# RWKV preparation: head sums as 64x64 products on four quarters of the array, transposes of the values after the gram products

## The chip, the cores and the metric

The program runs on one NeuronCore of one Trainium2 chip. A core has five engines with queues of their own: TensorE (PE in the profile; PEld are its weight loads), VectorE (DVE), ScalarE (ACT), GpSimd (POOL) and SyncE (SP), which starts most of the weight transfers. The metric is the device time of one execution in microseconds. The kernel before takes 837.95 us, the median of 3 runs (837.28 to 838.62).

## The reference

The program computes one decoder block on 512 tokens of width 1024, in float32: an attention sub-layer made of a sparse attention mixer and an RWKV-7 mixer side by side, and a gated MLP. The change touches the preparation of the RWKV mixer, which has 8 heads of 64 channels:

```python
w = -jax.nn.softplus(-(w0 + jnp.tanh(xw) @ w2)) - 0.5
decay = jnp.exp(-jnp.exp(w.astype(jnp.float32)))
a = jax.nn.sigmoid(a0 + xa @ a2)
...
kk = k * k_k.reshape(H, N).astype(jnp.float32)
kk = kk / jnp.maximum(jnp.sqrt(jnp.sum(kk * kk, axis=-1, keepdims=True)), 1e-12)
k = k * (1.0 + (a - 1.0) * k_a.reshape(H, N).astype(jnp.float32))
...
y = y + jnp.sum(r * k * r_k, axis=-1, keepdims=True) * v
```

Two of these lines sum over the 64 channels of a head: the norm of `kk`, and the bonus `sum(r * k * r_k)`, which multiplies `v`. These are the head sums.

## The kernel before

Activations are kept with channels on the partitions and the 512 tokens along the free dimension. A tile of 128 partitions therefore holds two heads, a *pair*; there are four pairs (`NH2 = 4`). Every weight is split into two parts, `whi` and `wlo` (ACT rounds `raw` to `whi`, DVE or POOL subtracts to get `wlo`), as is the normalised input (`hh`, `hl`), and a projection of 128 channels (`dense_fm`, L417) is 24 matmuls of 128x128 by 512 columns into one PSUM bank: `whi` with `hh` and `hl` eight times, then `wlo` with `hh` eight times.

For each pair `p` the preparation has these steps:

- `front(p)` (L495): the projection of the key; two small products `zw` and `za` (64 rows each, side by side in the array) for decay and `a`; `shift_mix` writes `kx`; then the running sum `cum` of the log decay inside each chunk of 64 tokens, and its exponentials `ep` and `pi`.
- `norms(p)` (L519): ACT squares `kx` into `kk`; TensorE multiplies `kk` by `ones`, a 128x128 matrix with two 64x64 blocks of ones on its diagonal, so that each partition receives the sum over its own head; DVE bounds it from below (`rn`), ACT takes logarithm and exponential, which makes 1/norm.
- `receptance(p)` (L531) and `values_of(p)` (L536): one projection each, into `rx` and `vx`. There is one buffer for `vx`.
- `values_tok(p)` (L541): four 128x128 transposes of `vx` on TensorE, and four copies by ACT into `UV` (values with tokens on the partitions).
- `vectors(p)` (L551): ten DVE instructions that build `AR`, `bh` and `tv`; TensorE sums `tv` over each head with the same `ones`, and DVE multiplies the sums by `vx` into `BO`.
- `gram(p)` (L570): sixteen transposes of `bh` into two banks, copied by ACT into `BKT`; then for each of eight chunks and both heads a product of `bh` with `AR`, masked by DVE into `AB`. The first four chunks go into one bank each of the tags `b` and `a`, the last four into two banks of the tag `mm`.

PSUM has eight banks: four with the tag `mm` (`mmb()`), two with `a` (`pa()`) and two with `b` (`pb()`). Tiles of one tag take their turns on its banks, so that a tile waits until the one before it on that bank has been read for the last time.

The loop at L597 to L609 works on two pairs at a time: `front` and `norms` of pair p+1, then `values_tok` and `vectors` of pair p, `receptance` of p+1, `gram` of p, `values_of` of p+1. Behind the third round comes one more projection (`kcp`). This part is not ordered by hand: a planner at compile time sets the order of each engine's queue, by the order of the program, by when it expects operands to be ready, and by free banks and buffers. `tc.high_priority()` moves the instructions in its block to the front of that choice. Other parts stand under `tc.manual_schedule`, which keeps the written order on the engines named.

After the loop DVE inverts the 32x32 diagonal blocks of all chunks (L625 to L636), a long run of dependent instructions, beside which TensorE makes the query and key projections. The chunk recurrence follows from L941 on; it uses products of 64x64 on all four quarters of the array (L951 and L954: `AR` with the state `M0` into the banks X and Y).

Of the kernel before, what the change touches and what calls it, by code (L numbers as in the profile page):

```python
# [13 lines left out]
AF = mybir.ActivationFunctionType  # L14
ALU = mybir.AluOpType
# [8 lines left out]
DH = 64  # L24
H = 8
NH2 = H // 2
# [54 lines left out]
def hybrid_block(ctx: ExitStack, tc: tile.TileContext, A: dict, out: bass.AP):  # L81
# [25 lines left out]
    def bank(tag, bufs, shape=(128, 512)):  # L107
        return ps.tile(list(shape), F32, name="ps_" + tag, tag=tag, bufs=bufs)

    def mmb():  # L110
        return bank("mm", 4)

    def pa():
        return bank("a", 2)

    def pb():
        return bank("b", 2)

    def mm(o, l, r, start, stop):
        te.matmul(o, lhsT=l, rhs=r, start=start, stop=stop)  # L120

    def act(o, i, f=AF.Copy, **kw):
        sc.activation(o, i, f, **kw)  # L123

    def tt(o, a, b, op):
        v.tensor_tensor(o, a, b, op=op)  # L126

    def ts(o, a, s1, s2, op0=ALU.mult, op1=ALU.add):
        if s2 is None:
            v.tensor_scalar(o, a, s1, None, op0=op0)  # L130
        else:
            v.tensor_scalar(o, a, s1, s2, op0=op0, op1=op1)

    def stt(o, a, s, b, op0=ALU.mult, op1=ALU.add):
        v.scalar_tensor_tensor(o, a, s, b, op0=op0, op1=op1)  # L135
# [3 lines left out]
    ident, mask, ones, cmask = kc[:, 0:128], kc[:, 128:256], kc[:, 256:384], kc[:, 384:416]  # L139
# [16 lines left out]
    for name in ("rwkv_mu", "rwkv_w0", "rwkv_a0", "rwkv_k_k", "rwkv_k_a", "rwkv_r_k", "rwkv_ln_g", "rwkv_ln_b"):  # L156
        r0, n = ROWS[name]
        src = A[name]
        if name == "rwkv_r_k":
            src = src.rearrange("l h d -> l (h d)")  # L160
# [3 lines left out]
    pt = pa()  # L164
# [3 lines left out]
    def col(name, i=0):  # L168
        r0, n = ROWS[name]
        return prm[:, r0 + i:r0 + i + 1]  # L170
# [37 lines left out]
    def norm_tiles(pool_):  # L208
        return (cp.tile([128, NT, 2], F32, name="ss", tag="ss"),
                [pool_.tile([128, D], F32, name="h", tag="h", bufs=NT) for _ in range(NT)])  # L210
# [123 lines left out]
    with tc.manual_schedule(engines={getattr(mybir.EngineType, e) for e in ("PE", "Activation", "DVE", "Pool")}):  # L334
# [37 lines left out]
        for k in range(KT):  # L372
# [5 lines left out]
            if k == 6:  # L378
                pt = pa()
# [37 lines left out]
    def dense_fm(xh, xl, kt=KT):  # L417
        return run(dense_fm_g(xh, xl, kt))
# [12 lines left out]
    UV = rp.tile([128, NCH, NH2, 2, DH], F32, name="UV")  # L431
    BO = gp.tile([128, 4, S], F32, name="BO", tag="BO")
# [11 lines left out]
    def shift_mix(p, m, dst):  # L444
        mu = col("rwkv_mu", m)
        act(dst, p, AF.Copy, scale=omm[:, m:m + 1])
        stt(dst[:, 1:], p[:, :-1], mu, dst[:, 1:])

    def t2(name, bufs=1):
        return tp.tile([128, S], F32, name=name, tag=name, bufs=bufs)  # L450
# [11 lines left out]
    for name, (r0, n) in ROWS.items():  # L462
        if r0 >= NR0:
            r0 -= NR0
            src = A[name]
            if name.startswith("cmp_pe"):
                src = src.rearrange("l a d -> l (a d)")
# [10 lines left out]
    def chunks(ap):  # L478
        return ap.rearrange("p (c t) -> p c t", t=C)
# [15 lines left out]
    def front(p):  # L495
        cs = slice(128 * p, 128 * p + 128)
        kx = t2("kx", 2)
        pk = dense_fm(hh, hl)
        zw, za = pa(), pb()
        mm(zw, wa[0:64, cs], xw[0:64], True, True)  # L500
        mm(za, wa[64:128, cs], xw[64:128], True, True)
        shift_mix(pk, 4 + p, kx)
        cl = t2("cl")
        act(cl, zw, AF.Tanh, scale=0.5, bias=w0h[:, p:p + 1])
        aa = t2("aa", 2)
        act(aa, za, AF.Tanh, scale=0.5, bias=a0h[:, p:p + 1])
        ts(cl, cl, -0.5 * DECAY, -0.5 * DECAY)
        cum = t2("cum")
        v.tensor_tensor_scan(out=cum, data0=scanm.rearrange("p c t -> p (c t)"), data1=cl, initial=0.0,
                             op0=ALU.mult, op1=ALU.add)  # L510
        ep = tp.tile([128, NCH, C + 1], F32, name="ep", tag="ep", bufs=2)
        v.memset(ep[:, :, 0:1], 1.0)
        act(ep[:, :, 1:], chunks(cum), AF.Exp)
        pi = t2("pi", 2)
        act(pi, cum, AF.Exp, scale=-1.0)
        v.tensor_copy(PC[:, p, :, None], ep[:, :, C:C + 1])
        L[p] = dict(kx=kx, aa=aa, ep=ep, pi=pi)

    def norms(p):  # L519
        kx = L[p]["kx"]  # L520
        kk = t2("kk", 2)
        act(kk, kx, AF.Square, scale=col("rwkv_k_k", p))
        ss = pa()
        mm(ss, ones, kk, True, True)
        rn = t2("rn", 2)
        ts(rn, ss, 1e-24, None, op0=ALU.max)
        act(rn, rn, AF.Ln)
        act(rn, rn, AF.Exp, scale=-0.5)
        L[p].update(kk=kk, rn=rn)

    def receptance(p):  # L531
        rx = t2("rx", 2)
        shift_mix(dense_fm(hh, hl), p, rx)
        L[p]["rx"] = rx

    def values_of(p):  # L536
        vx = t2("vx")
        shift_mix(dense_fm(hh, hl), 8 + p, vx)
        L[p]["vx"] = vx

    def values_tok(p):  # L541
        vx = L[p]["vx"]
        pt = pb()
        for i in range(4):
            te.transpose(pt[:, 128 * i:128 * i + 128], vx[:, 128 * i:128 * i + 128], ident)
        for r in range(2):
            for cc in range(2):
                act(UV[64 - 64 * r:128 - 64 * r, cc::2, p, r, :],
                    pt[64 * cc:64 * cc + 64].rearrange("p (c r d) -> p c r d", r=2, d=DH)[:, :, r, :])

    def vectors(p):  # L551
        kx, aa, ep, pi, kk, rn, rx, vx = (L[p][k] for k in ("kx", "aa", "ep", "pi", "kk", "rn", "rx", "vx"))
        stt(AR[:, p, :, 1, :], chunks(rx), 1.0, ep[:, :, 1:], ALU.mult, ALU.mult)
        stt(kk, kx, col("rwkv_k_k", p), rn, ALU.mult, ALU.mult)
        stt(AR[:, p, :, 0, :], chunks(kk), -1.0, ep[:, :, 0:C], ALU.mult, ALU.mult)
        stt(kk, aa, 1.0, kk, ALU.add, ALU.mult)
        bh = tp.tile([128, NCH, 3, C], F32, name="bh", tag="bh")
        stt(bh[:, :, 0, :], chunks(kk), 0.5, chunks(pi), ALU.mult, ALU.mult)
        v.tensor_copy(bh[64:128, :, 2, :], bh[64:128, :, 0, :])
        ts(aa, aa, kah[:, p:p + 1], oma[:, p:p + 1])  # L560
        stt(kx, kx, 1.0, aa, ALU.mult, ALU.mult)
        stt(bh[:, :, 1, :], chunks(kx), 1.0, chunks(pi), ALU.mult, ALU.mult)
        tv = t2("tv")
        stt(tv, rx, col("rwkv_r_k", p), kx, ALU.mult, ALU.mult)
        L[p]["bh"] = bh
        bs = pa()
        mm(bs, ones, tv, True, True)
        tt(BO[:, p], bs, vx, ALU.mult)

    def gram(p):  # L570
        bh = L[p]["bh"]
        ptr = [pb(), pa()]
        for c in range(NCH):
            for r in range(2):
                rs = slice(64 * r, 64 * r + 64)
                te.transpose(ptr[r][:, 64 * c:64 * c + 64], bh[rs, c, r:r + 2].rearrange("p a t -> p (a t)"),
                             ident[rs, rs])
        for r in range(2):
            act(BKT[:, :, p, r, :], ptr[r].rearrange("p (c j) -> p c j", c=NCH))
        for c0 in range(0, NCH, 4):  # L580
            ptr = [mmb(), mmb()] if c0 else [pb(), pa()]
            for i in range(4):
                for r in range(2):
                    rs = slice(64 * r, 64 * r + 64)
                    mm(ptr[r][:, 128 * i:128 * i + 128], bh[rs, c0 + i, r:r + 2].rearrange("p a t -> p (a t)"),
                       AR[rs, p, c0 + i].rearrange("p a t -> p (a t)"), True, True)
            for r in range(2):
                tt(AB[:, c0:c0 + 4, p, r, :], ptr[r].rearrange("p (c t) -> p c t", c=4),
                   mask[:, None, :].to_broadcast([128, 4, 128]), ALU.mult)


    front(0)
    norms(0)
    receptance(0)
    values_of(0)
    late_params()
    for p in range(NH2):  # L597
        if p + 1 < NH2:
            front(p + 1)
            norms(p + 1)  # L600
        values_tok(p)
        vectors(p)
        if p + 1 < NH2:
            receptance(p + 1)
        gram(p)
        if p + 1 < NH2:
            values_of(p + 1)
        if p + 2 == NH2:
            kcp = dense_fm(hh, hl)  # L609
# [15 lines left out]
    for g in range(2):  # L625
        for b in range(2):
            r = 64 * g + 32 * b
# [75 lines left out]
    pt = pa()  # L703
# [31 lines left out]
    for b in (1, 0):  # L735
        for g in range(2):
            r = 64 * g + 32 * b
# [511 lines left out]
    for m in range(KT):  # L1249
        cs = slice(128 * m, 128 * m + 128)  # L1250
# [13 lines left out]
    ss, hs = norm_tiles(ntp)  # L1264
# [36 lines left out]
    with tc.manual_schedule(engines=KTS):  # L1301
        for t in range(NT):
            qs = slice(128 * t, 128 * t + 128)
            p = mmb()
# [13 lines left out]
        for pair in range(2):  # L1318
            cs = slice(256 * pair, 256 * pair + 256)
# [37 lines left out]
    for hf in range(2):  # L1357
        bo = dense_tok(512, aT[:, 0], aT[:, 1], NF)
        for t in range(NT):
            n = 256 if hf and t == NT - 1 else 512  # L1360
            for c0 in range(0, 512, n):
                cs = slice(512 * hf + c0, 512 * hf + c0 + n)
# [30 lines left out]
```

## Time and profile before

| | us |
|---|---|
| median of 3 runs | 837.95 |
| the profiled execution | 837.93 |
| its span, first to last instruction | 836.1 |
| TensorE busy | 822.2 |
| DVE busy | 514.2 |
| ACT busy | 406.7 |
| POOL busy | 52.4 |

All durations in rows are those of the one profiled execution. A row of the order of time has the start (us from the span's start), the busy time, the engine, the line of the code, the operation, the tile written and the tiles read, and shapes; `x8` at its end merges eight instructions. A float32 matmul appears as two instructions, since it makes two passes; the dense products, in the rounded type, appear as one. Matmul lines are those of the helper `mm` (L120), DVE and ACT lines often those of `tt` (L126), `ts` (L130), `stt` (L135) and `act` (L123), so the tiles' names tell the instructions apart. `ps_a`, `ps_b` and `ps_mm` are the banks by tag; `kc` is the constant tile that holds `ones` and the identity. A row that groups instructions has their number, their busy time, the mean of one in ns, and the engine's idle time before them with what ended it.

### The profile page before, as it was taken

The page shows a single profiled execution, that of the slowest core. Times are in us where ns is not written, and L with a number is a line of the kernel's source. Part 1 is how long each engine was busy: PE and PEld are TensorE (multiplying, and loading weights), DVE is VectorE, ACT ScalarE, POOL GpSimd, SP SyncE. Part 2 cuts the span into 40 slices and gives each one's busy share as a digit, 9 for nine tenths or more (in the row PEclk, how much of TensorE's full clock was granted, in tenths as well). Part 3 has the DMA queues.
Part 4 walks back from the last instruction along what each step waited for, and adds up shares of the span by engine and source line. Part 5 has one row for each costly group of instructions (what it writes and reads, how often), then busy time and mean ns, then how long its engine had stood idle before and what let it go on. Part 6 is the DMA issues. An engine that isn't in the chain of part 4 may idle for free.

```text
span 836.1 us, 12860 instructions
## 1 busy us (share of the span) xinstructions
PE 822.2 (98%) x5097; PEld 667.1 (80%) x5097; DVE 514.2 (62%) x998; ACT 406.7 (49%) x792; POOL 52.4 (6%) x69
## 2 busy tenths in 40 slices
PE   7999999999999999999999999999999999999998
PEld 5777778887787876777788988888888888888886
DVE  4478779973565778787664665666555666322222
ACT  6766654463555777676334454444444444221210
POOL 5200020140000100111000000000000000000000
PEclk9999999999999999999999999999999999999999
DMA  7432222346452310000275033332333332223421
GB/s 228 116 78 75 76 76 77 72 125 182 116 114 77 83 45 13 26 26 26 64 249 179 1 101 100 101 99 87 93 101 101 100 101 91 88 100 114 139 75 51
DMA packets 109104, 78.73 MB, mean 94 GB/s; under 512 B 3869, under 2 KB 97748, under 8 KB 109044
## 3 DMA queue, kind: packets, MB, share of 16 engines
q1 hardware_dynamic: 106512, 73.51, 30.4%
q10 hardware_dynamic: 1060, 2.55, 1.0%
q0 software_dynamic: 1472, 1.86, 1.0%
q8 instruction: 40, 0.66, 0.3%
q14 instruction: 20, 0.16, 0.1%
HBM read 74.56 MB, written 2.29 MB: 92 GB/s over the span
## 4 chain that ended last, share of the span: by engine, by line
PE 53%; DVE 0%; DVEq 0%; issue 0%
PE ps_mm L120 52%; PE ps_a L203 0%; PE ps_b L203 0%; PE ps_a L120 0%; PE ps_b L1197 0%; PE ps_mm L1197 0%; DVE x L126 0%; DVEq L1389 0%; PE ps_a L1149 0%
## 5 line engine op out<-in xcount | busy, mean ns | idle before, releaser
L299 DVE TENSOR_TENSOR wlo<-raw,whi 128x1024 fp32r<-128x1024 f32 (+1 forms) x111 | 131.5, 1186 | 184.8 <-PE ps_mm L120 157.2
L120 PE MATMUL ps_mm<-hh,whi 128*128 128x512 f32 (+1 forms) x624 | 242.6, 391 | 0.6 <-ACT whi L123 0.5
L120 PE MATMUL ps_mm<-hl,whi 128*128 128x512 f32 (+1 forms) x624 | 240.4, 387 | 0.0
L123 ACT ACTIVATE whi<-raw 128x1024 fp32r<-128x1024 f32 (+3 forms) x124 | 123.3, 996 | 165.2 <-PE ps_mm L120 143.9
L120 PE MATMUL ps_mm<-hh,wlo 128*128 128x512 f32 (+1 forms) x624 | 151.7, 384 | 0.0
L120 PEld LDWEIGHTS ps_mm<-hh,whi 128*128 128x128 f32 x624 | 117.3, 188 | 27.3 <-issue 1.3
L120 PEld LDWEIGHTS ps_mm<-hl,whi 128*128 128x128 f32 x624 | 117.4, 188 | 23.4 <-issue 1.0
L120 PEld LDWEIGHTS ps_mm<-hh,wlo 128*128 128x128 f32 x624 | 115.1, 188 | 23.3
L120 PE MATMUL ps_mm<-whi,aT 128*128 128x512 f32 x352 | 84.5, 390 | 0.0
L120 PEld LDWEIGHTS ps_mm<-whi,aT 128*128 128x128 f32 x352 | 65.9, 188 | 14.3 <-issue 0.4
L135 DVE SCALAR_TENSOR_TENSOR cgv<-ps_mm,cw,cgv 128x511 f32<-128x511 f32 (+1 forms) x88 | 65.4, 746 | 1.6
L123 ACT ACTIVATE cgv<-ps_mm,cw 128x512 f32<-128x512 f32 x44 | 34.2, 779 | 23.3 <-PE ps_mm L120 23.3
L120 PE MATMUL ps_mm<-wlo,aT 128*128 128x512 f32 x176 | 44.3, 389 | 0.0
L123 ACT ACTIVATE P<-P,nm 128x512 f32<-128x512 f32 (+3 forms) x64 | 35.3, 553 | 14.9 <-DVE nm L1171 14.9
L123 ACT ACTIVATE aT<-cgv 128x512 fp32r<-128x512 f32 x22 | 13.9, 632 | 56.8 <-DVE cgv L126 56.8
L120 PEld LDWEIGHTS ps_mm<-wlo,aT 128*128 128x128 f32 x176 | 33.0, 188 | 6.9
L123 ACT ACTIVATE cgv<-cgv 128x512 f32<-128x512 f32 x22 | 13.9, 632 | 41.0 <-DVE cgv L135 41.0
L299 POOL TENSOR_TENSOR wlo<-raw,whi 128x512 fp32r<-128x512 f32 (+3 forms) x13 | 20.5, 1573 | 202.2 <-PE ps_mm L120 148.2
L1171 DVE CUSTOM_DVE_ANT_0 P<-ps_a,AB 128x512 f32<-128x512 f32 (+3 forms) x64 | 29.4, 485 | 4.2 <-PE ps_a L120 3.7
L126 DVE TENSOR_TENSOR x<-x,ps_mm 128x512 f32<-128x512 f32 (+1 forms) x17 | 11.1, 655 | 23.6 <-PE ps_mm L120 22.0
L126 DVE TENSOR_TENSOR aT<-cgv,aT 128x512 fp32r<-128x512 f32 x22 | 15.2, 693 | 14.7 <-ACT aT L123 14.7
L120 PE MATMUL ps_a<-KH,qst 128*128 128x512 f32 (+3 forms) x64 | 21.3, 348 | 1.6 <-DVE nm L1171 0.9
(358 smaller groups left out, 1199.1 us busy)
## 6 DMA issues: line engine op xcount, KB each, us to landing
raw<-in_w_up_dram SPq DMA_DIRECT2D x44, 512.0 KB, 3.8
raw<-in_w_in_dram SPq DMA_DIRECT2D x38, 512.0 KB, 3.9
raw<-in_w_down_dram SPq DMA_DIRECT2D x22, 512.0 KB, 3.6
raw<-in_w_out_dram SPq DMA_DIRECT2D x8, 512.0 KB, 3.5
xt<-in_x_dram SPq DMA_DIRECT2D x4, 512.0 KB, 5.9
raw<-in_cmp_w_v_dram SPq DMA_DIRECT2D x4, 512.0 KB, 3.8
raw<-in_w_proj_b_dram SPq DMA_DIRECT2D x8, 256.0 KB, 2.7
raw<-in_w_proj_a_dram SPq DMA_DIRECT2D x8, 256.0 KB, 2.7
```

The lines of the kernel that those rows point to most:

```text
L120: te.matmul(o, lhsT=l, rhs=r, start=start, stop=stop)
L123: sc.activation(o, i, f, **kw)
L126: v.tensor_tensor(o, a, b, op=op)
L135: v.scalar_tensor_tensor(o, a, s, b, op0=op0, op1=op1)
L299: eng.tensor_tensor(lo, raw, hi.bitcast(F32), op=ALU.subtract)
L1171: v.tensor_tensor_reduce(out=P[:, i], in0=sp[:, N * (i - i0):N * (i - i0) + N], in1=BT[:, h, 384 - 128 * qt:512], scale=-1.0, scalar=-NEG, ...
```

## The change

A head sum becomes four products. `head_sums` takes one bank of each tag, `a` and `b`. For the first half of the tokens (256 columns, i = 0) the 64 rows of each head are multiplied by a 64x64 block of ones into the same half of the partitions, in the first bank; for the second half (i = 1) into the other half of the partitions, in the second bank. So the sums of the second half stand on the partitions of the other head, and everything that reads them crosses over: `EXCH` lists the three copies (destination partitions, source partitions, half). In `norms` the bound is applied by two DVE instructions into `kk`, the logarithm is taken there, and the exponential is written in three pieces into `rn`. In `vectors` the product with `vx` is made in three pieces.

`values_tok(p)` moves from before `vectors(p)` to behind `gram(p)`, and its four copies into `UV` get high priority.

```diff
         v.tensor_copy(PC[:, p, :, None], ep[:, :, C:C + 1])
         L[p] = dict(kx=kx, aa=aa, ep=ep, pi=pi)
 
+
+
+    def head_sums(src):
+        o = [pa(), pb()]
+        for i in range(2):
+            for r in range(2):
+                a, b = slice(64 * r, 64 * r + 64), slice(64 * (r ^ i), 64 * (r ^ i) + 64)
+                mm(o[i][b, 0:256], ones[a, a], src[a, 256 * i:256 * i + 256], True, True)
+        return o
+
+    EXCH = [(slice(0, 128), slice(0, 128), 0), (slice(0, 64), slice(64, 128), 1), (slice(64, 128), slice(0, 64), 1)]
+
     def norms(p):
         kx = L[p]["kx"]
         kk = t2("kk", 2)
         act(kk, kx, AF.Square, scale=col("rwkv_k_k", p))
-        ss = pa()
-        mm(ss, ones, kk, True, True)
+        ss = head_sums(kk)
         rn = t2("rn", 2)
-        ts(rn, ss, 1e-24, None, op0=ALU.max)
-        act(rn, rn, AF.Ln)
-        act(rn, rn, AF.Exp, scale=-0.5)
+        for i in range(2):
+            ts(kk[:, 256 * i:256 * i + 256], ss[i][:, 0:256], 1e-24, None, op0=ALU.max)
+        act(kk, kk, AF.Ln)
+        for d, s_, i in EXCH:
+            cs = slice(256 * i, 256 * i + 256)
+            act(rn[d, cs], kk[s_, cs], AF.Exp, scale=-0.5)
         L[p].update(kk=kk, rn=rn)
 
     def receptance(p):
@@ -543,10 +557,11 @@
         pt = pb()
         for i in range(4):
             te.transpose(pt[:, 128 * i:128 * i + 128], vx[:, 128 * i:128 * i + 128], ident)
-        for r in range(2):
-            for cc in range(2):
-                act(UV[64 - 64 * r:128 - 64 * r, cc::2, p, r, :],
-                    pt[64 * cc:64 * cc + 64].rearrange("p (c r d) -> p c r d", r=2, d=DH)[:, :, r, :])
+        with tc.high_priority():
+            for r in range(2):
+                for cc in range(2):
+                    act(UV[64 - 64 * r:128 - 64 * r, cc::2, p, r, :],
+                        pt[64 * cc:64 * cc + 64].rearrange("p (c r d) -> p c r d", r=2, d=DH)[:, :, r, :])
 
     def vectors(p):
         kx, aa, ep, pi, kk, rn, rx, vx = (L[p][k] for k in ("kx", "aa", "ep", "pi", "kk", "rn", "rx", "vx"))
@@ -563,9 +578,10 @@
         tv = t2("tv")
         stt(tv, rx, col("rwkv_r_k", p), kx, ALU.mult, ALU.mult)
         L[p]["bh"] = bh
-        bs = pa()
-        mm(bs, ones, tv, True, True)
-        tt(BO[:, p], bs, vx, ALU.mult)
+        bs = head_sums(tv)
+        for d, s_, i in EXCH:
+            cs = slice(256 * i, 256 * i + 256)
+            tt(BO[d, p, cs], bs[i][s_, 0:256], vx[d, cs], ALU.mult)
 
     def gram(p):
         bh = L[p]["bh"]
@@ -597,12 +613,13 @@
     for p in range(NH2):
         if p + 1 < NH2:
             front(p + 1)
+        if p + 1 < NH2:
             norms(p + 1)
-        values_tok(p)
         vectors(p)
         if p + 1 < NH2:
             receptance(p + 1)
         gram(p)
+        values_tok(p)
         if p + 1 < NH2:
             values_of(p + 1)
         if p + 2 == NH2:
```

## The prediction

> **What bounds the kernel now.** I read the page's busy table first, then the chain that ended last, then busy time by windows over the preparation, and last the order of time on TensorE around every instruction that the change touches.
>
> ```profile
> span 836.1 us, 12860 instructions
> PE 822.2 (98%) x5097; PEld 667.1 (80%) x5097; DVE 514.2 (62%) x998; ACT 406.7 (49%) x792; POOL 52.4 (6%) x69
> PE 53%; DVE 0%; DVEq 0%; issue 0%
> ```
>
> TensorE is busy for 822.2 of 836.1 us, and the chain that ended last is TensorE alone for the 53% of the span that it covers. A microsecond of TensorE work taken out anywhere should shorten the run by a microsecond, as long as another engine doesn't become late by it.
>
> ```profile
> core 0: us, PE busy (x) PEld busy (x) DVE busy (x) ACT busy (x) POOL busy (x), PEclk, DMA share, GB/s
> 67.90:90.40 22.50, 22.50 (x134) 17.17 (x133) 17.21 (x27) 14.47 (x21) 0.00 (x0) 1.00 0.27 71
> 90.40:112.90 22.50, 22.50 (x134) 17.20 (x133) 17.18 (x26) 14.48 (x21) 0.00 (x0) 1.00 0.26 71
> 112.90:122.00 9.10, 8.71 (x63) 6.54 (x63) 6.33 (x10) 4.28 (x8) 2.35 (x1) 1.00 0.22 58
> 165.00:172.00 7.00, 7.00 (x160) 6.02 (x159) 6.87 (x5) 3.80 (x8) 2.23 (x2) 1.00 0.26 77
> ```
>
> One visit of a pair takes 22.50 us and TensorE never stops in it; DVE has 5.3 us free and ACT 8.0. Only in the last pair (112.9 to 122.0) does TensorE idle. DVE then inverts the blocks and is full (6.87 of 7.00 in the last window), but that starts when the last gram product is out, so it moves with TensorE. DMA is at a quarter.
>
> **The head sums now.** Eight of them run, two a pair. In the visits before pairs 1, 2 and 3 the sum for `kk` of the next pair and the sum for `tv` of this pair stand next to each other, in the middle of a dense projection:
>
> ```profile
> 99.33 0.40 PE L120 MATMUL ps_mm<-hh,whi 128*128 128x512 f32 x1
> 99.56 1.02 PE L120 MATMUL ps_a<-kk,kc 128*128 128x512 f32 x2
> 100.42 1.02 PE L120 MATMUL ps_a<-tv,kc 128*128 128x512 f32 x2
> 100.88 0.79 PE L120 MATMUL ps_mm<-hl,whi 128*128 128x512 f32 x1
> 101.51 0.40 PE L120 MATMUL ps_mm<-hh,whi 128*128 128x512 f32 x1
> ```
>
> Matmul ends are modelled, so I go by starts. A dense product takes 0.23 us (99.33 to 99.56). A float32 head sum is two passes of 512 columns: 0.86 us (99.56 to 100.42), 0.43 a pass. The two end where the next dense product really begins, 101.51 − 0.23 = 101.28: together 1.72 us, with no loss at either edge.
>
> **The head sums after.** Each becomes four products of 64x64, one on each quarter of the array, of 256 columns: the diagonal quarters into one bank, the crossed quarters into another. The kernel already has this pattern in its chunk recurrence, at 64 columns: `AR` with `M0` into X (diagonal, ps_b) and into Y (crossed, ps_a).
>
> ```profile
> 194.25 0.39 PE L120 MATMUL ps_mm<-hl,whi 128*128 128x512 f32 x1
> 194.57 0.27 PE L120 MATMUL ps_b<-M,AR 64*64 64x64 f32 x2
> 194.59 0.27 PE L120 MATMUL ps_a<-M,AR 64*64 64x64 f32 x2
> 194.68 0.22 PE L120 MATMUL ps_b<-M,AR 64*64 64x64 f32 x2
> 195.03 0.22 PE L120 MATMUL ps_b<-M,AR 64*64 64x64 f32 x2
> 195.20 0.50 PE L120 MATMUL ps_mm<-hh,whi 128*128 128x512 f32 x1
> 195.53 0.39 PE L120 MATMUL ps_mm<-hl,whi 128*128 128x512 f32 x1
> ```
>
> The four quarters start within 0.02 us of each other, and from 194.68 to 195.03 come six rounds of four: 0.058 us a round. One pass of 64 columns at the head sum's rate would take 0.43 / 8 = 0.054, so all four quarters stream at once, with 8% lost at this short length. For 256 columns a round is 0.215 (half of 0.43) to 0.233 (the same 8%); I take 0.22, since a fixed loss weighs less in a longer pass. A head sum is two rounds, 0.44 us.
>
> The array has to change its shape, though, and the same rows price that. The dense product before ends at 194.25 + 0.23 = 194.48, the next begins at 195.53 − 0.23 = 195.30: 0.82 us for eight rounds that stream in 8 x 0.054 = 0.43. So 0.39 us goes for getting into the shape and out again, and I take half of it for each way. The weight loads, two for each product, are in these rounds too.
>
> Here the Trainium skill speaks against the change: TensorEngine Tiling (Array Packing), section Restrictions and Gotchas, says that different row tiles cannot access the same PSUM bank at the same time. The diagonal products of one head sum are two row tiles in one bank. The rows show two row tiles filling one bank (ps_b, x2) with starts inside 0.02 us, on different partitions of it, so the trace doesn't agree for this pattern; what the rule would cost is the second rival.
>
> **The sum.** First, the three visits with adjacent sums: now 1.72, after four rounds and one change of shape, 4 x 0.22 + 0.39 = 1.27. Saved 0.45 each, **1.35** in all. Bounds: 0.86 each if the change of shape is hidden, 0.06 each if the two sums come apart and each pays its own (1.72 − 0.88 − 0.78).
>
> Second, the lone `kk` sum of pair 0:
>
> ```profile
> 34.07 0.40 PE L120 MATMUL ps_mm<-hh,whi 128*128 128x512 f32 x1
> 34.61 1.13 PE L120 MATMUL ps_a<-kk,kc 128*128 128x512 f32 x2
> 35.80 0.39 PE L120 MATMUL ps_mm<-hh,whi 128*128 128x512 f32 x1
> ```
>
> TensorE is free at 34.30 and starts at 34.61, when ACT has squared `kx`. The wait covers the way into the shape. From 34.61 to 35.57 are 0.96 us; after, 0.44 + 0.20 = 0.64. Saved **0.32** (bounds 0 and 0.52).
>
> Third, the last pair, where the transposes of the values now stand before its `tv` sum:
>
> ```profile
> 116.49 1.97 PE L120 MATMUL ps_mm<-hh,wlo 128*128 128x512 f32 x8
> 118.73 0.66 PE L545 MATMUL ps_b<-kc,vx 128*128 128x128 f32 x4 [0.26 <-DVE vx L135]
> 119.22 1.02 PE L120 MATMUL ps_a<-tv,kc 128*128 128x512 f32 x2
> 121.02 0.37 PE L120 MATMUL ps_b<-AR,bh 64*128 64x128 f32 x1
> 123.00 0.50 PE L120 MATMUL ps_mm<-whi,hh 128*128 128x512 f32 x1
> 123.57 0.40 PE L120 MATMUL ps_mm<-whi,hh 128*128 128x512 f32 x1
> 124.15 0.50 PE L120 MATMUL ps_mm<-whi,hh 128*128 128x512 f32 x1 [0.18 <-DVE AB L126]
> 116.13 0.74 DVE L135 SCALAR_TENSOR_TENSOR tv<-rx,prm,kx 128x512 f32<-128x512 f32 x1
> 117.93 0.74 DVE L135 SCALAR_TENSOR_TENSOR vx<-ps_mm,prm,vx 128x511 f32<-128x511 f32 x1
> 120.28 0.69 DVE L126 TENSOR_TENSOR BO<-ps_a,vx 128x512 f32<-128x512 f32 x1 [1.61 <-PE ps_a L120]
> L126 DVE TENSOR_TENSOR BO<-ps_a,vx 128x512 f32<-128x512 f32 x4 | 2.8, 692 | 2.1 <-PE ps_a L120 2.1
> L126 DVE TENSOR_TENSOR M<-M,ps_a 128x256 f32<-128x256 f32 x2 | 0.8, 422 | 2.1 <-PE ps_a L120 2.0
> L967 DVE COPY UV<-ps_b 64x256 f32<-64x256 f32 x4 | 1.7, 428 | 5.7 <-ACT UV L123 5.7
> ```
>
> The dense work ends at 116.49 + 8 x 0.23 = 118.33. TensorE then waits for `vx` until 118.73, transposes it, and only then sums `tv`, which was ready at 116.87. After the change the sum starts at once: 118.33 + 0.10 + 0.44 = 118.87. The first gram products wait for the sums' banks, which `BO` empties: now one DVE instruction of 0.69 that begins 0.20 after the sum (119.22 + 0.86 to 120.28) and ends at 120.97, 0.05 before the gram product at 121.02. After, `BO` is three instructions of about 0.43 (the rows of 128x256 and 64x256), from 119.07 to 120.36, and the gram products start at 120.41, 0.61 earlier. The transposes then follow and take 0.49 (118.73 to 119.22), so the query projection begins 0.12 earlier. It meets a wait now: 124.15 is 0.35 later than a start 0.23 after 123.57, and some 0.10 more follows as the pipeline restarts, for a bank that DVE empties behind the gram products. These run 0.61 earlier and the projection only 0.12, so that 0.45 goes. Saved **0.57**, bounds 0 (the wait stays and `BO` is slower) and 1.06 (the transposes fall into a wait).
>
> What is added elsewhere lies beside TensorE. DVE gets one more instruction for the maximum (2 x 0.42 for 0.69) and two for `BO` (3 x 0.43 for 0.69): 0.75 us a visit, against 5.3 free. ACT writes `rn` in three pieces:
>
> ```profile
> L123 ACT ACTIVATE UV<-ps_b 64x256 f32<-64x256 f32 x20 | 7.5, 375 | 1.9 <-PE ps_b L545 1.7
> L123 ACT ACTIVATE rn<-rn 128x512 f32<-128x512 f32 x8 | 5.1, 632 | 0.1
> 98.24 0.72 ACT L123 ACTIVATE kk<-kx,prm 128x512 f32<-128x512 f32 x1
> ```
>
> 3 x 0.375 for 0.632 is 0.49 a visit, against 8.0 free; without that cover it would cost these amounts, 1.24 a visit, some 5 in all. In the pairs before the last the rest of the projection stands between the sums and the gram products and hides the longer `BO`. The four `UV` copies (4 x 0.375 = 1.5) move from before the logarithm to behind the gram products. The transposes of the other pairs only change their place, inside dense work of the same array shape: 0. No DMA is added or moved.
>
> 1.35 + 0.32 + 0.57 = **2.24 us**. The profiled execution took 837.93 us (span 836.1 and 1.8 around it), the median of the three runs is 837.95; 837.95 − 2.24 = 835.7.
>
> **The rivals.** *The sums come apart.* The order outside the hand-ordered parts is a planner's, and the two sums stand together only because both became ready to it there. With their own banks in two tags they may not. Then 3 x 0.06 + 0.32 + 0.57 = 1.07: 836.9. For it: the `tv` sum's data is ready long before. Against it: they stood together in all three visits.
>
> *Two row tiles in one bank take turns.* The second product of a head sum then waits for the first; the third, in the other bank, runs beside the second; the fourth waits again: three turns instead of one round, 2 x 3 x 0.22 = 1.32 a head sum. An adjacent pair takes 2.64 + 0.39 = 3.03 for 1.72, 1.31 lost three times; pair 0 takes 1.52 for 0.96, 0.56 lost; at the end `BO` is 0.88 later than in my sum, which turns 0.57 saved into 0.31 lost. 3.93 + 0.56 + 0.31 = 4.8: 842.7, slower. The place is the second product of each head sum, and it decides as soon as that starts a pass (0.2) behind the first. Against it stand the recurrence rows; for it only that their passes are a quarter as long.
>
> *TensorE arrives too early.* The transposes stood before the dense work that hides ACT's square. That ends at 98.96, 0.60 before the sum at 99.56; with 0.49 less in front 0.11 is left. If the planner also puts two dense products fewer ahead, TensorE waits 0.35 in three visits, of which 0.10 covers the way into the shape: 2.24 − 0.75 = 1.5, so 836.5.
>
> **Numbers.** About 0.2% (1.7 us) is what a measurement of this kernel can tell from no change. My forecast 0.60 (0.50 of it faster by more than that, 0.10 within), apart 0.15 (within), early 0.07 (0.05 within, 0.02 faster), turns 0.08 (slower), and 0.10 for a plan that changes elsewhere, 0.04 faster, 0.01 within, 0.05 slower. Faster 0.56, same 0.31, slower 0.13. All upper bounds together (2.6 + 0.52 + 1.06 = 4.2) give 833.8, which is unlikely; the low end takes three quarters of that, 834.8. The high end takes in the sums apart and a small loss elsewhere: 838.4. The turns stay outside.
>
> **What would show it.** Right: rows of 64*64 with 64x256 whose four first starts lie within 0.05 us, 1.2 to 1.4 us for two adjacent sums, the last pair's `tv` sum directly behind the dense work, the next dense stage some 2 us earlier. Wrong: starts 0.2 apart, single head sums of 0.8 us between dense products, TensorE idle before a sum or before the gram products in pairs 0 to 2, a visit of 22.5 us.

## The result and the profile after

| | before | after |
|---|---|---|
| median | 838.07 us (837.28 to 838.62, 6 runs) | 843.03 us (842.10 to 843.65, 6 runs) |
| ratio | | 1.0062 [1.0052, 1.0073] |
| profiled execution, its span | 837.93, 836.1 | 843.65, 841.9 |

The changed kernel is slower by 5.0 us, where 2.2 us less was forecast, and lies outside the range. Its six executions fall into two groups, 842.10 to 842.53 at a mean granted clock of 1.000 and 843.53 to 843.65 at 0.998; the profiled one is of the second, and the median lies between them. The page of the changed kernel has, for the first two lines shown of before:

```profile
span 841.9 us, 12979 instructions
PE 822.6 (98%) x5145; PEld 667.7 (79%) x5145; DVE 516.3 (61%) x1010; ACT 409.8 (49%) x800; POOL 52.5 (6%) x69
```

TensorE's busy time is what it was (822.6 for 822.2), and the span is 5.8 longer: TensorE waits. The view of waits, for TensorE from 45 to 135 us, says for what (total, times, longest):

```profile
PE ps_b L559 <- ACT BKT L123: 5.3, 3, 2.3
PE ps_b L120 <- DVE BO L126: 0.7, 1, 0.7
PE ps_mm L120 <- ACT QK L123: 0.4, 1, 0.4
PE ps_a L120 <- ACT kk L123: 0.3, 1, 0.3
```

L559 is the transposes of the values at their new place. The windows show the visits that had no idle time before (22.50 of 22.50):

```profile
45.00:67.90 22.90, 20.30 (x132) 15.18 (x131) 18.19 (x33) 13.87 (x22) 0.00 (x0) 0.94 0.27 70
67.90:90.40 22.50, 21.01 (x140) 15.95 (x139) 15.16 (x26) 14.30 (x21) 0.00 (x0) 0.99 0.27 71
90.40:112.90 22.50, 21.01 (x141) 16.00 (x140) 16.74 (x28) 14.34 (x22) 0.00 (x0) 1.00 0.25 68
```

TensorE stands still for 1.49 us in the second and third, and for 2.60 in the first, where the granted clock (behind POOL) is lower as well. ACT is busy for 14.3 of 22.5, no more than before (14.5).

**The head sums** came out as worked out. TensorE's order of time in visit 2:

```profile
80.41 0.39 PE L120 MATMUL ps_mm<-hh,whi 128*128 128x512 f32 x1
80.73 0.43 PE L120 MATMUL ps_a<-kk,kc 64*64 64x256 f32 x2
80.74 0.43 PE L120 MATMUL ps_b<-kk,kc 64*64 64x256 f32 x2
81.00 0.38 PE L120 MATMUL ps_a<-kk,kc 64*64 64x256 f32 x2
...
81.21 0.38 PE L120 MATMUL ps_a<-tv,kc 64*64 64x256 f32 x2
...
81.44 0.38 PE L120 MATMUL ps_b<-tv,kc 64*64 64x256 f32 x2
81.75 0.50 PE L120 MATMUL ps_mm<-hl,whi 128*128 128x512 f32 x1
82.09 0.40 PE L120 MATMUL ps_mm<-hh,whi 128*128 128x512 f32 x1
```

Both sums still stand together. Each `x2` here is the two quarters that share a bank, and the two banks' quarters start 0.01 us apart; from the end of the dense product before (80.41 + 0.23) to the real start of the one behind (82.09 − 0.23) 1.22 us pass, for 1.72 before.

**The wait** comes behind the gram products. TensorE, then ACT, in the same visit:

```profile
86.42 1.06 PE L120 MATMUL ps_mm<-AR,bh 64*128 64x128 f32 x16
88.96 0.66 PE L559 MATMUL ps_b<-kc,vx 128*128 128x128 f32 x4 [1.49 <-ACT BKT L123]
89.38 0.48 PE L120 MATMUL ps_mm<-hh,whi 128*128 128x512 f32 x1
```

```profile
81.15 0.61 ACT L123 ACTIVATE pi<-cum 128x512 f32<-128x512 f32 x1
82.26 1.28 ACT L123 ACT_TABLE_LOAD   x1 [0.50 <-DVE kk L130]
83.55 0.63 ACT L123 ACTIVATE kk<-kk 128x512 f32<-128x512 f32 x1
84.09 1.04 ACT L123 ACTIVATE whi<-raw 128x1024 fp32r<-128x1024 f32 x1
85.15 1.28 ACT L123 ACT_TABLE_LOAD   x1
86.44 1.27 ACT L123 ACTIVATE rn<-kk 128x256 f32<-128x256 f32 x3
87.74 0.69 ACT L123 ACTIVATE rx<-ps_mm,omm 128x512 f32<-128x512 f32 x1
88.32 0.59 ACT L123 ACTIVATE BKT<-ps_b 128x512 f32<-128x512 f32 x1
```

The transposes of `vx` need a bank of the tag `b`. It still holds the transposes of `bh`, which ACT copies to `BKT`. That copy was ready soon after the last of these transposes, which starts at 85.41, but ACT takes its instructions in order, and ahead of it stand a table load, the logarithm, a weight rounding, a second table load, the three-piece exponential and `rx`, back to back from 82.26 to 88.3. The dense product at 89.38, which needs nothing of all this, stands behind the transposes in TensorE's queue. So TensorE stops.

Followed along the profiled execution, the starts of the same instruction in both traces show where the 5.7 us of span come from:

| first start of | before | after | difference |
|---|---|---|---|
| `zw`/`za` of pair 1 | 50.98 | 50.60 | −0.38 |
| transposes of `bh`, pair 0 | 59.87 | 58.95 | −0.92 |
| `zw`/`za` of pair 2 | 73.45 | 76.94 | +3.49 |
| transposes of `bh`, pair 1 | 82.34 | 84.92 | +2.58 |
| `zw`/`za` of pair 3 | 95.93 | 100.47 | +4.54 |
| transposes of `bh`, pair 2 | 104.81 | 108.46 | +3.65 |
| query projection | 123.00 | 128.45 | +5.45 |
| first state product of the recurrence | 194.57 | 200.47 | +5.90 |
| end of the span | 836.12 | 841.86 | +5.74 |

From `zw`/`za` to the transposes of `bh` visits 2 and 3 gain some 0.90: the 0.49 of the transposes, which are gone from there, and 0.41 from the sums. Behind it, the same visits lose 0.49 for the transposes and 1.49 waiting. Visit 1 loses 4.41 there: 0.49, a wait of 2.32, and the rest to TensorE's clock, as its order of time and the windows from 64 to 70 us show:

```profile
63.83 0.66 PE L559 MATMUL ps_b<-kc,vx 128*128 128x128 f32 x4 [2.32 <-ACT BKT L123]
...
65.02 0.55 PE L120 MATMUL ps_mm<-hl,whi 128*128 128x512 f32 x1
65.37 0.63 PE L120 MATMUL ps_mm<-hh,whi 128*128 128x512 f32 x1
...
68.36 0.47 PE L120 MATMUL ps_mm<-hl,whi 128*128 128x512 f32 x1
68.66 0.39 PE L120 MATMUL ps_mm<-hh,whi 128*128 128x512 f32 x1
```

```profile
64.00:66.00 2.00, 2.00 (x10) 1.68 (x10) 2.00 (x5) 1.71 (x5) 0.00 (x0) 0.77 0.18 52
66.00:68.00 2.00, 2.00 (x6) 1.51 (x6) 2.00 (x4) 0.07 (x1) 0.00 (x0) 0.50 0.00 0
68.00:70.00 2.00, 2.00 (x9) 1.65 (x8) 1.99 (x5) 0.22 (x1) 0.00 (x0) 0.87 0.04 8
```

Between 65.37 and 68.36 dense products start 0.43 us apart instead of 0.23, at a granted clock of 0.50. From 65.02 to 68.66 are nine of them: 3.64 us for 9 x 0.23 = 2.07, so 1.57 lost. 0.49 + 2.32 + 1.57 = 4.38, all but 0.03 of it. The wait is longer than in the other visits because ACT's first table load comes later there: 6.52 after `zw`/`za` (57.12 − 50.60) for 5.32 in visit 2 (82.26 − 76.94), as the squaring of `kx` waits 0.93 for DVE. That is 1.20 more on ACT's side; TensorE itself is 0.38 later there, and 1.20 − 0.38 = 0.82 is the difference of the two waits but for 0.01. Why DVE is late in this visit was not followed.

### The profile page after: what moved, and what is told of

It reads as the page before. It is cut to its first block, busy times and chain, and to the rows that moved or that the text cites. A ratio compares the mean times of both kernels' runs of the same rounds, so it can differ in the third digit from the quotient of the medians.

```text
span 841.9 us, 12979 instructions
## 1 busy us (share of the span) xinstructions
PE 822.6 (98%) x5145; PEld 667.7 (79%) x5145; DVE 516.3 (61%) x1010; ACT 409.8 (49%) x800; POOL 52.5 (6%) x69
## 4 chain that ended last, share of the span: by engine, by line
PE 53%; DVE 0%; DVEq 0%; issue 0%
PE ps_mm L120 52%; PE ps_b L203 0%; PE ps_a L203 0%; PE ps_a L120 0%; PE ps_b L1214 0%; PE ps_mm L1214 0%; DVE x L126 0%; DVEq L1406 0%; PE ps_a L1166 0%
## 5 line engine op out<-in xcount | busy, mean ns | idle before, releaser
L120 PEld LDWEIGHTS ps_mm<-whi,aT 128*128 128x128 f32 x352 | 65.9, 188 | 14.3 <-issue 0.4
L120 PE MATMUL ps_mm<-whi,hh 128*128 128x280 f32 (+2 forms) x72 | 22.7, 335 | 0.5 <-ACT QK L123 0.4
```

## The experiments

**The theory.** ACT's queue in order makes the loss: between the `kk` sum and the copies that empty banks for TensorE stands a chain that the change lengthens (two bound pieces on DVE ahead of it, three exponential pieces in it) while TensorE reaches its end earlier. The rivals were that the moved transposes cost that much by themselves, or the products of 64x64.

**The two halves of the change alone.** First the new sums, with `values_tok` and its copies as before:

```diff
-        with tc.high_priority():
-            for r in range(2):
+        for r in range(2):
...
             norms(p + 1)
+        values_tok(p)
         vectors(p)
...
         gram(p)
-        values_tok(p)
```

> The new head sums alone; the transposes of the values and their copies stand where they stood before the change. Theory A (the loss is the wait of the moved transposes for the bank that ACT's BKT copy empties): no such wait, so near the kernel before. Here the transposes fall between the two head sums of a visit, so that each sum pays its own change of array shape: 0.06 us saved a visit, 0.3 at pair 0, 0.3 lost at the last pair: 837.9 us, 837.0 to 838.6. Theory B (the loss comes from the sums: more and shorter instructions on DVE and ACT, products that slow TensorE): most of the 5 us lost is here, 841 us or more.

Measured: 844.51 us (844.17 to 844.73, 5 runs), 1.0082 [1.0068, 1.0096]. The expected 837.9 was missed, and by the time alone this is what was expected if the sums themselves lose (841 or more). TensorE's largest wait in this run, and in visit 2 the copies and the product that waits for them:

```profile
PE ps_b L120 <- ACT UV L123: 4.1, 3, 1.4
```

```profile
86.39 0.77 ACT L123 ACTIVATE UV<-ps_b 64x256 f32<-64x256 f32 x2
87.22 0.37 PE L120 MATMUL ps_b<-AR,bh 64*128 64x128 f32 x1 [1.44 <-ACT UV L123]
```

`values_tok` stands at its old place in the program, but its transposes fall between the two sums, 4.38 us after `zw`/`za` (80.38 − 76.00) for 1.06 in the kernel before (74.51 − 73.45): the new sums displace them without the edit to the loop. Of the four `UV` copies that empty their bank three end up behind a table load, two behind the exponential. Their bank is needed next by the gram products, which wait 1.27 to 1.44 in each visit. It is the same queue, with another bank hanging on it. TensorE's waits from 45 to 135 us come to 5.6 us in this run, for 0.5 before; the rest of the 6.6 by which its span is longer was not followed. So this run doesn't acquit the products of 64x64 yet; the last one below does.

Then the move alone, with the sums of before:

```diff
-        ss = head_sums(kk)
+        ss = pa()
+        mm(ss, ones, kk, True, True)
...
-        bs = head_sums(tv)
+        bs = pa()
+        mm(bs, ones, tv, True, True)
```

> The move alone, with the head sums as they were. Theory A: TensorE waits before the transposes of pairs 0 to 2 until ACT has copied BKT, but for less than with the new sums, since ACT's exponential is one instruction (0.64 us less) and TensorE arrives 0.45 us later: some 0.7 us three times, 0.5 gained at the last pair: 839.6 us, 838.5 to 841. Theory B: 837.5 to 838.2, no loss.

Measured: 837.60 us (836.94 to 838.03, 11 runs), 0.9997 [0.9989, 1.0006]: nothing. ACT and then TensorE in visit 2, in order of time:

```profile
77.98 0.61 ACT L123 ACTIVATE pi<-cum 128x512 f32<-128x512 f32 x1
78.61 1.28 ACT L123 ACT_TABLE_LOAD   x1
...
82.92 0.63 ACT L123 ACTIVATE rn<-rn 128x512 f32<-128x512 f32 x1
...
84.03 0.59 ACT L123 ACTIVATE BKT<-ps_b 128x512 f32<-128x512 f32 x1
```

```profile
83.77 1.06 PE L120 MATMUL ps_mm<-AR,bh 64*128 64x128 f32 x16
84.76 0.66 PE L545 MATMUL ps_b<-kc,vx 128*128 128x128 f32 x4
```

The copy ends at 84.62 and the transposes start at 84.76: the move has no wait by a margin of 0.14 us. The theory's own number (839.6) missed this: it counted the shorter exponential and TensorE's later arrival, and left out that ACT's chain starts earlier here than in the changed kernel. Counted from `zw`/`za` of the visit (73.77 here, 76.94 in the changed kernel), the first table load starts at 4.84 here and at 5.32 there: here it follows `pi` at once, there it follows DVE's second bound piece, 0.48 later. The exponential takes 1.27 there instead of 0.63, another 0.64. And TensorE ends the gram products at 10.99 here and, with the wait taken off (88.96 − 1.49 − 76.94), at 10.53 there. 0.48 + 0.64 + 0.46 − 0.14 = 1.44, against the wait of 1.49 in this visit. So each half of the change spoils the other: the sums use up the margin that the move lives on.

**Another bank for the transposes.** The changed kernel, with their bank from the tag `mm`:

```diff
-        pt = pb()
+        pt = mmb()
```

> The changed kernel, with the transposes of the values in a bank of the tag mm (four banks, the next of them free) in place of tag b. Theory A: the wait of 2.3, 1.5 and 1.5 us is gone, the granted clock of the profile is back at 1.000, and what was predicted of the sums comes out: 836.0 us, 835.3 to 836.9. Theory B: 842 to 843, as the changed kernel.

Measured: 843.07 us (842.16 to 844.08, 5 runs), 1.0065 [1.0053, 1.0078]: no gain. The wait moved by one instruction:

```profile
PE ps_mm L120 <- DVE rx L135: 4.4, 3, 2.0
```

Now the dense products behind the transposes wait, for the bank from which ACT and DVE make `rx`, and `rx` stands behind the same exponential. So it isn't this one bank; the next bank that ACT has to empty is late as well.

**The chain shortened.** Two kernels leave out the logarithm and the exponential of the norms, in the changed kernel and in the one before, so that `rn` only holds a bounded sum:

```diff
-            ts(kk[:, 256 * i:256 * i + 256], ss[i][:, 0:256], 1e-24, None, op0=ALU.max)
-        act(kk, kk, AF.Ln)
...
+            ts(rn[:, 256 * i:256 * i + 256], ss[i][:, 0:256], 1e-24, 0.002, op0=ALU.max, op1=ALU.min)
```

> The changed kernel without the logarithm and the exponential of the norms: DVE writes the bounded sums into rn, so ACT loses two table loads and four instructions a visit (1.28 + 0.63 + 1.28 + 1.27 = 4.5 us); the norm of kk is left out of the computation. Theory A (ACT's queue between the kk sums and the BKT copies sets the wait; the new sums lengthen it and reach its end earlier): the waits are gone and the predicted time comes out: 835.8 us, 835.0 to 836.9. Theory C (the order of the transposes and the turns of the banks cost what they cost, ACT is only the name on the wait): 840 us or more.

> The kernel before without the logarithm and the exponential of the norms (left out as in e5). TensorE waited for nothing on that queue before the change, except at the last pair. Theory A: 837.4 us, 836.6 to 838.0, and e5 is 1.0 to 2.2 us faster than this. Theory C: 837.4, and e5 slower by 3 us or more.

Measured: 836.74 us (836.35 to 837.63, 11 runs) and 838.20 (837.92 to 838.77, 11 runs). The changed kernel gains 6.3 us by it and no wait for `BKT` is left; the kernel before gains nothing. Without the chain the change is a gain of 1.46 us. Some 0.6 of that is three waits for `kk` that only the second of the two kernels has, which came out 0.2 above its expected range.

A third kernel only makes the exponential one instruction of 512 columns again; the norms of the second half aren't crossed back:

```diff
-        for d, s_, i in EXCH:
-            cs = slice(256 * i, 256 * i + 256)
-            act(rn[d, cs], kk[s_, cs], AF.Exp, scale=-0.5)
+        act(rn, kk, AF.Exp, scale=-0.5)
```

> The changed kernel with the exponential as one instruction of 512 columns (0.63 in place of 1.27 us); the second half of the norms is not crossed back to its own head, so that part of the result is that of the other head. Theory A: each of the three waits is 0.64 shorter: 841.1 us, 840.0 to 841.6. Theory C: no difference, 843.

Measured: 839.06 us (838.51 to 839.43, 11 runs), 4.0 below the changed kernel. More than expected, for two reasons that the waits and the window from 66 to 68 us of this run show:

```profile
PE ps_b L557 <- ACT BKT L123: 2.5, 3, 1.1
```

```profile
66.00:68.00 2.00, 2.00 (x11) 1.65 (x10) 1.98 (x5) 1.06 (x1) 0.00 (x0) 1.00 0.00 0
```

The waits fall by 2.8, and the clock stays at 1.00 behind a first wait of 1.10 instead of 2.32, which saves the 1.57 that the profiled execution of the changed kernel lost. The two add up to 4.37, and the two profiled executions differ by 843.65 − 839.28 = 4.37. That they agree so closely is partly chance, as the 0.27 for `kk` in visit 1, gone here too, isn't counted.

A fourth takes another piece out of ACT's queue: DVE makes the first scaling of `rx`, in the changed kernel and, for comparison, in the kernel before.

```diff
-        shift_mix(dense_fm(hh, hl), p, rx)
+        pr = dense_fm(hh, hl)
+        ts(rx, pr, omm[:, p:p + 1], None)
+        stt(rx[:, 1:], pr[:, :-1], col("rwkv_mu", p), rx[:, 1:])
```

> The changed kernel with one edit: the first scaling of rx is made by DVE, so that ACT's queue is 0.69 us shorter between the kk sums and the BKT copies, and nothing else of the sums, the move or the banks changes. Theory A: each wait is 0.69 shorter, the first stays under the length at which TensorE's clock fell, as with one exponential: 839.2 us, 838.3 to 840.3. Theory C (order and banks, not ACT): 843.

> The kernel before with the first scaling of rx by DVE. TensorE waited for nothing on ACT there, so nothing is gained but at the last pair, where DVE is 0.69 fuller: 837.7 us, 837.0 to 838.2. If the shorter ACT queue is worth something by itself: below 837.

Measured: 839.71 us (838.93 to 839.98, 11 runs) for the changed kernel, 3.3 less, and 837.15 (836.83 to 837.60, 11 runs), 0.9994 [0.9985, 1.0003], for the one before: only where the queue is waited for does an instruction less in it count.

**The wait taken off TensorE's way.** Next the transposes of pair p go into the projection of the values of pair p+1, between its products and the instruction that overwrites `vx`; the last pair's stay behind its gram products:

```diff
     def values_of(p):
+        pv = dense_fm(hh, hl)
+        if p:
+            values_tok(p - 1)
         vx = t2("vx")
-        shift_mix(dense_fm(hh, hl), 8 + p, vx)
+        shift_mix(pv, 8 + p, vx)
...
         gram(p)
-        values_tok(p)
         if p + 1 < NH2:
             values_of(p + 1)
+        else:
+            values_tok(p)
```

> The changed kernel, with the transposes of pair p issued behind the 24 products of the next pair's value projection (before its result is written over vx), in the same bank of tag b. Theory A: 5.4 us of dense work cover ACT's way to the BKT copy, no wait: 836.0 us, 835.3 to 837.0. If a free bank is not what they wait for but the values themselves or the planner's order, e4 would still be slow or e3 would. Theory B: 842 to 843.

Measured: 838.62 us (837.99 to 840.46, 11 runs), 1.0013 [1.0005, 1.0022]. Better than the change by 4.4, but not the gain expected. TensorE's waits:

```profile
PE ps_b L120 <- DVE BO L126: 1.6, 1, 1.6
PE ps_a L120 <- ACT kk L123: 0.7, 3, 0.3
```

The wait for `BKT` is gone, and TensorE reaches the gram stage of the last pair 1.62 us earlier than before (118.55 for 120.17). There it waits 1.61 for `BO`: DVE works through one chain from `rx` to `vx`, `rx` comes from ACT behind the longer exponential, and the chain starts 0.75 later than before (108.26 for 107.51). What TensorE gained in three visits, it loses at the one place where DVE's chain is the bound. The three waits for `kk`, 0.7 in all, are the rival "TensorE arrives too early".

So both were changed on top of this: DVE scales `rx`, as above, and the first four chunks' gram products take the `mm` banks, which don't wait for `BO`.

```diff
-            ptr = [mmb(), mmb()] if c0 else [pb(), pa()]
+            ptr = [pb(), pa()] if c0 else [mmb(), mmb()]
```

> e9 without the swap of the gram products' banks (transposes behind the projection, rx scaled by DVE). If e4's loss at the last pair was the wait of the gram products for BO's banks: slower than e9 by 0.5 to 1.2 us, 836.5. If the earlier rx alone removed it: 835.7.

> The changed kernel with three edits: the transposes behind the next pair's value projection (as e4), the first scaling of rx by DVE in place of ACT (0.69 us out of ACT's queue, and DVE need not wait for it), and the gram products of the first four chunks in banks of the tag mm, so that they need not wait for BO. Theory A: the 1.6 us that e4 lost at the last pair are gone, the vectors of the last pair are ready some 0.7 earlier: 836.6 us, 835.6 to 837.6. If DVE's extra 0.69 a visit counts, or the chain through DVE at the last pair doesn't get shorter: 838.6, as e4.

Measured: 836.57 us (835.96 to 837.03, 11 runs) without the exchange of banks and **835.64 (834.98 to 835.93, 8 runs), 0.9974 [0.9964, 0.9984]** with it. This beats both kernels, by 0.3% over the one before. In its trace TensorE is busy for all of each visit again, and the one wait left from 45 to 135 us is 0.88 for the copies to `QK`, in the query projection. The window of visit 2:

```profile
67.90:90.40 22.50, 22.50 (x148) 17.23 (x147) 18.95 (x31) 14.98 (x24) 0.00 (x0) 1.00 0.26 71
```

**The sums by themselves.** Last, the same kernel with the sums of before (the edit to the sums is the one shown for the move alone):

> e9 with the head sums as before the change (full 128x128 products, one instruction each for the bound, the exponential and BO). Theory A: with the waits out of the way the new sums are worth what the product rows gave, 3 x 0.45 + 0.3: e9 is 1.7 us faster than this, so 837.3, 836.7 to 838.0. If e9's gain comes from its other edits, this is as fast as e9 or faster: 835.6 or less.

Measured: 837.45 us (837.12 to 838.29, 11 runs), 0.9996 [0.9987, 1.0005]. In its trace, too, `QK` is all that TensorE waits for from 45 to 135 us. Where the preparation doesn't wait for ACT, the products of 64x64 are worth 837.45 − 835.64 = 1.81 us, against 1.35 + 0.32 = 1.67 in the prediction's sum for the visits and pair 0. So the products themselves are not what loses.

## Why the prediction was wrong

**The adjacent sums** (0.45 each) held: 0.50 by the rows, 0.41 by the stage. The quarters of one bank don't take turns, so the second rival, whose 842.7 lies nearest to the result, has the number by chance; its place, a second product that starts 0.2 late, isn't there: the two sums take 1.22 us, where turns would make its 3.03.

**The lone sum of pair 0** (0.32) held: from `zw`/`za` of pair 0 to those of pair 1 the changed kernel gains 0.26 (50.98 − 31.53 before, 50.60 − 31.41 after).

**The step that failed** is the one that priced the move at nothing: "The transposes of the other pairs only change their place, inside dense work of the same array shape: 0." The prediction followed the transposes by TensorE's time and by their operand, `vx`, and never asked for their bank. At the new place they need a bank that ACT empties last of all, and stand ahead of dense products that need nothing. Measured, the 0 is 5.3 us of waiting and, in the profiled execution, 1.57 us lost at half the clock. None of the signs named for a wrong prediction covers this place: they look for idle time before the sums and before the gram products, and it lies behind the gram products. Yet the move alone does cost nothing (837.60), by its margin of 0.14 us. The 0 failed together with a second one.

**The same error in the second place** is "What is added elsewhere lies beside TensorE": the pieces of ACT and DVE were weighed against the free time of a visit (8.0 and 5.3 us). 8.0 was true as a mean, and is so after the change; between the first table load and the `BKT` copies there is none. There was none before either: in visit 3 of the kernel before ACT works without a break of more than 0.03 us from the first row here to the end of the last (107.97):

```profile
101.95 1.28 ACT L123 ACT_TABLE_LOAD   x1
...
106.79 0.69 ACT L123 ACTIVATE rx<-ps_mm,omm 128x512 f32<-128x512 f32 x1
107.38 0.59 ACT L123 ACTIVATE BKT<-ps_b 128x512 f32<-128x512 f32 x1
```

The price of the three pieces, 3 x 0.375 − 0.632 = 0.49, was fair (1.27 − 0.63 = 0.64 measured), but it lay on the path, in three visits. That the four `UV` copies leave ACT's queue ahead of this chain was seen, and not that this is what made room for the move: with the move alone the first table load starts 1.18 earlier after `zw`/`za` than before (4.84 for 101.95 − 95.93 = 6.02, and for as much in visit 2). The prediction did name what these pieces would cost without cover, "some 5 in all", and kept it out of its range. That the loss is 5.0 is in part chance: a visit's 1.49 is 0.48 and 0.64 on ACT's side, 0.46 from TensorE's earlier arrival, and the margin.

**The last pair** (0.57) was right in its first two pieces and wrong in its third. TensorE's order of time there, after the change:

```profile
122.10 1.98 PE L120 MATMUL ps_mm<-hh,wlo 128*128 128x512 f32 x8
...
126.05 0.37 PE L120 MATMUL ps_b<-AR,bh 64*128 64x128 f32 x1 [0.74 <-DVE BO L126]
...
128.45 0.48 PE L120 MATMUL ps_mm<-whi,hh 128*128 128x512 f32 x1
...
133.00 0.50 PE L120 MATMUL ps_mm<-whi,hh 128*128 128x512 f32 x1 [0.43 <-ACT QK L123]
```

From the end of the dense work (122.10 + 8 x 0.23 = 123.94) to the gram products pass 2.11 us, for 2.69 before: 0.58 earlier, predicted 0.61. The query projection starts 0.16 earlier by the same count, predicted 0.12. But the 0.45 that its wait for `AB` cost was not gained, and the `UV` copies now stand in ACT's queue ahead of the copies to `QK`, so that the projection waits 0.43 for these. From its start to the recurrence 0.45 is lost (5.90 − 5.45), so that the term, 0.57 in the sum, came out as 0.16 − 0.45 = −0.29.

**The rival "TensorE arrives too early"** is there in one of its three visits: in visit 1 the sums wait 0.27 for `kk`. It explains 0.3 of the 5 us.

## What to carry to other kernels

When an instruction is moved within an in-order queue, price it by the bank or buffer that it takes at the new place and by what stands ahead of the one who empties it, not by its operands alone; if it has to wait, everything behind it pays. Free time of an engine as a mean over a stage says nothing about the stretch between two named instructions: count that stretch. And an edit that frees time on the bounding engine brings it earlier to every place where another engine hands something over, so the margins there have to be known before the gain is booked.

## What the runs showed that was not expected

- In the profiled execution a wait of 2.32 us on TensorE is followed, some 1.2 us after its work resumes, by a stretch at a granted clock of 0.50. By the three windows above (0.77, 0.50 and 0.87) it is about 3.4 us long, and it costs 1.57 us. The profiled execution with the `mm` bank has the same behind a wait of 2.04 (0.50 from 66 to 68 us). It doesn't come each time: by the mean clock of 0.998 three of the six executions of the changed kernel have it, and these take 1.3 us longer on average than the other three; with the `mm` bank two of five have that clock. After waits of 1.61, 1.49 and 1.10 the traces show nothing of the kind. Two of the 11 executions with the transposes in the projection (840.14 and 840.46) have a clock of 0.997 and 0.998 too, without a trace to say where. The Trainium skill (TensorE: Matmul & The Clock Gate, Part 1) has the clock at half after an idle window of about 3.4 us, with windows that run free of the kernel. The half clock and a stretch of about one window agree with the trace; the gap that sufficed here was shorter. What decides whether an execution has the stretch was not tried.
- With the sums of before and the move alone, the first table load starts at 78.61 in visit 2, while DVE still writes the bound that the logarithm reads (78.53 to 79.22); in the changed kernel it waits for the bound (`[0.50 <-DVE kk L130]`). Why the load waits in the one and not in the other was not settled; it is 0.48 of the 1.49.
